# A decoder block on one core: row squares and the FFN's first weights queued behind copies out of PSUM, and layer two's loads queued three products sooner

## The chip, the core and the metric

The kernel runs on one core of a Trainium2 chip. A core has TensorE (matmuls, results in PSUM, eight banks), VectorE (DVE), ScalarE (ACT), GpSimd (POOL) and SyncE (SP), each working through its own queue in order; here nearly all DMAs are issued from SP's queue. PEld is TensorE's loading of the stationary operand, which overlaps its matmuls. The metric is device time of the whole program in microseconds (us), lower is better.

## The reference

One decoder block over 2048 tokens of width 1024, in float32:

```python
hn = rmsnorm(h, norm1_g)
proj = hn @ w_in                       # u_pool | q | k | v, 512 each
y_pool = pool_mixer(u_pool, ...)       # causal means over 2, 4, 8, 16 tokens, then 128x128 maps
o = stick_breaking_attention(q, k, v)  # 8 heads of 64, strictly causal
mixed = concat(rmsnorm(y_pool, pool_out_g), rmsnorm(o, attn_out_g))
h = h + mixed @ w_out
hn2 = rmsnorm(h, norm2_g)
h = h + square(relu(hn2 @ w_up)) @ w_down   # 1024 -> 4096 -> 1024
return rmsnorm(h, final_g)
```

## The kernel before, in words

Tokens are cut into four tiles j = 0 to 3 of T = 512 columns; features lie on the 128 partitions. Every matmul operand is split into a high and a low part (`split`: ScalarE copies the rounded high part, VectorE subtracts for the low part), and each product is three matmuls of 128x512: high-high, high-low, low-high.

The program has these stages:

- **The front** (to some 485 us): two passes over pairs of tiles do the input projection (`in_proj`, `dense`, 24 matmuls for each block of 128 output features, weights `raw` split into `hl` up to five pieces ahead), the pooling mixer and the attention of recent keys. `dense` has two PSUM banks, `pd`; `evac` copies or adds the result out of the bank, on ScalarE or VectorE, and `done` remembers the last two such instructions: `done[1]` is the newest. Copies of v are `vf`, which TensorE then transposes (`ptv`). Attention runs in units woven between the dense products: logits `pz` (two banks), `sh` and `sg` (sigmoids on ScalarE, out of `pz`), a mask by GpSimd, a scan and products on VectorE, transposes `pta`, a split `at`, context matmuls `po`.
- **The squares of x's rows.** The first norm needs mean squares of x's rows. For tiles 1 to 3 they are taken by `row_sums`: a load of 128 rows into the one buffer `rlast`, then a ScalarE square that adds up the row. Four for a tile, twelve in all. For tile 1 all are asked for at once (`n` is 5). For tiles 2 and 3 one step is asked for ahead of an input projection; a step is the square of the last rows and the load of the next.
- **Output projection** (first addition at 487.0 us, last at 672.5): for each tile eight blocks c of 24 matmuls; `add_acc` adds the bank to `acc` on VectorE. At c = 3 of the last tile, `begin_ffn` opens the FFN's buffers and starts `up`.
- **FFN, layer one** (`up`, TensorE's first product at 672.31): Strassen's scheme with seven products P1 to P7 for each pair of halves, 12 matmuls each; stationary operands `hw` from weights `rb` and their sums `rt`, moving operands `sa` from loads `sr` (three buffers) of sums kept in DRAM. `post` brings results out, stores activations to `sd` and sums to `sdi`. Product P2 ends with the store of block A11, P7 with that of A22, P4 with that of S3.
- **FFN, layer two** (`down`, first product at 1285.31): steps of 24 or 48 matmuls; a step loads weights `wr` and one or two operands `ar` and splits them into `wd` and `ad`. `make_ahead` writes steps ahead of their use, up to six operands. Buffers of `ar` are five, two in a pool that the first steps share.

The order on each engine is made by a scheduler that simulates the program as it is written. It may draw an instruction forward wherever its data allow it. `tc.issue_after(ins)` adds an edge without a semaphore: what is written in the block and runs on the same engine as `ins` stays behind `ins` in that engine's queue; on another engine it has no effect. `last_split[0]` is the VectorE half of the newest weight split, `done[1]` may be on either engine, and `marks["A11"]`, `["A22"]` and `["S3"]` are DMAs in SP's queue.

Of the kernel before, what the change touches and what calls it, by code (L numbers as in the profile page):

```python
# [19 lines left out]
NT = S // T  # L20
# [25 lines left out]
def hymba_block(ctx: ExitStack, tc: tile.TileContext, xT, x_rows, gains, w_in, pool_w, w_out, w_up, w_down, out):  # L46
# [110 lines left out]
    marks, gates = {}, []  # L157
    raws, grans, last_split, last_mm, last_load = [], [], [None], [None], [None]
    done = [None, None]
# [168 lines left out]
    def note(emit):  # L328
        prog.append((0, emit, False))
# [53 lines left out]
    def row_sums(j):  # L383

        x = rlast.rearrange("p x t -> p (x t)")
        for b in range(TB + 1):
            if b:
                nc.scalar.activation(x, x, AF.Square, accum_out=sums1[:, j - 1, b - 1:b])
            if b < TB:
                nc.sync.dma_start(x, x_rows[j, b])  # L390
            yield

    row_steps = [iter(())] + [row_sums(j) for j in range(1, NT)]

    def sum_rows(j, n=1):
        for _ in range(n):
            next(row_steps[j])

    def norm1_rms(j):
        st[j]["ss"] = sums1[:, j - 1]  # L400
# [144 lines left out]
    def drained(j):  # L545
        while j not in finished:
            state["due"] = 0.0
            advance(0.1)
# [69 lines left out]
    def tail(first):  # L618

        def root(j):  # L620

            if not (first and j < 2):
                drained(j)
                st[j]["todo"] = attn_norm(j, lambda: make_h(j))

        def mixes(j):
            load_mix(j, KD if first and j < 2 else 4)
            if "todo" in st[j]:
                st[j]["amix"] = st[j].pop("todo")()

        def begin(j):
            catch_up(len(later))
            st[j]["m"] += st[j].pop("amix", [])
            if j > 0:
                norm2(j - 1)
            if j == 2:
                sums_first()

        if first:
            note(to_out)  # L640
        else:
            note(lambda: (root(0), mixes(0), load_acc(0)))
        for j in range(NT):
            if j == 2 and first:
                note(to_last)
            note(lambda j=j: begin(j))
            for c in range(KD):
                if c == 0 and j == 0 and not first:
                    note(lambda: root(1))
                if c == 0 and j + 1 < NT:  # L650
                    note(lambda j=j: mixes(j + 1))
                if c == (2 if j == 0 else 4) and j + 2 < NT:
                    note(lambda j=j: root(j + 2))
                if c == 0 and j == 2:
                    note(lambda j=j: load_acc(j))
                if c == 4 and j in (0, 2):
                    note(lambda j=j: load_acc(j + 1))
                if c == 3 and j == NT - 1:
                    note(begin_ffn)
                wlist.append(w_out[c])  # L660
                step(2, lambda w, j=j, c=c: dense(j, "m", w, lambda ps: add_acc(j, c, ps)))

# [248 lines left out]
    A11, A12, A22, S1, S2, S3, S4 = range(7)  # L911
# [19 lines left out]
    def up(pools, more):  # L931
# [49 lines left out]
        def load(q, m):  # L981
            if q and m % (NM // 2) == NM // 2 - 1:
                raw[q, m] = raw[0, m]
                return
            raw[q, m] = (rbb if m >= NM // 2 else rba).tile([P, 4, G, P], F32, tag="rb", name="rb")
            nc.sync.dma_start(raw[q, m], w_up[m])
# [9 lines left out]
        def make_weights(g):  # L996
            q, m, s = slots[g]
            which, i = what[s][1]
            if s == "P2":
                add_weights(q, m)  # L1000
            hl = hlp.tile([P, 2, G, P], F32R, tag="hw", name="hw", align_bytes=256)
            split((hl[:, 0], hl[:, 1]), (sums if which else raw)[q, m][:, i])
            ops[g] = hl
# [85 lines left out]
        def post(q, m, s):  # L1089
            k = keep.setdefault((q, m), {})  # L1090
            x, y, z = (ps.get((q, m, b)) for b in "XYZ")
            new = lambda name: avp.tile([P, T], F32, tag="av", name=name)

            def put(i, t, kept=None):
                if q == 0 or m >= NM // 2 or i not in INNER:
                    kept = nc.sync.dma_start(sd[q][i][m // 2][:, m % 2], t)
                if q and i in INNER:
                    inner_sums(m, i, t)
                return kept

            def act_of(i, src, t):
                nc.scalar.activation(t, src, AF.Relu)  # L1102
                nc.scalar.activation(t, t, AF.Square)
                k[i] = t

            def copy(name):
                k[name] = pup.tile([P, T], F32, tag=name, name=name)
                nc.scalar.activation(k[name], y, AF.Copy)  # L1108

            if s == "P1":  # L1110
                copy("p1")
            elif s == "P2":
                t = new("a11")
                nc.vector.tensor_tensor(t, x, k["p1"], ALU.add)
                act_of(A11, t, t)
                put(A11, t)
            elif s == "P6":
                if q and m != NM // 2 - 1:
                    for i in INNER:
                        inner_row(m, i)  # L1120
                copy("u2")
            elif s == "P7":
                if q and m == NM // 2 - 1:
                    for i in INNER:
                        inner_row(m, i)
                copy("u3")
                t = new("a22")
                nc.vector.tensor_tensor(t, z, k["u3"], ALU.add)
                act_of(A22, t, t)
                marks["A22"] = put(A22, t)  # L1130
            elif s == "P4":
                t = new("a21")
                act_of("A21", y, t)
                k[S1] = new("s1")
                nc.vector.tensor_tensor(k[S1], t, k[A22], ALU.add)
                put(S1, k[S1])
                k[S2] = new("s2")
                nc.vector.tensor_tensor(k[S2], k[S1], k[A11], ALU.subtract)
                put(S2, k[S2])
                nc.vector.tensor_tensor(t, k[A11], t, ALU.subtract)  # L1140
                marks["S3"] = put(S3, t)
            elif s == "P3":
                t = new("a12")
                nc.vector.tensor_tensor(t, z, k["u2"], ALU.add)  # L1144
                act_of(A12, t, t)
                put(A12, t)
                s4 = new("s4")
                nc.vector.tensor_tensor(s4, t, k[S2], ALU.subtract)
                put(S4, s4)
                while waiting:  # L1150
                    inner_sums(*waiting.pop(0))

        load(*cols[0])
        make_weights(0)
        make_left(0, "P1")
        make_left(0, "P2")
# [9 lines left out]
        for g, (q, m, s) in enumerate(slots):  # L1166
# [7 lines left out]
            n = cols.index((q, m))  # L1174
# [6 lines left out]
            t, w = ps[q, m, bank], ops.pop(g)  # L1181
# [12 lines left out]
            if g + UA < len(slots):  # L1194
                make_weights(g + UA)
                q2, m2, s2 = slots[g + UA]
                n = cols.index((q2, m2)) + 2
# [3 lines left out]
    def down(pools):  # L1201
# [306 lines left out]
        def make_ahead(limit=len(steps)):  # L1508

            while ahead[0] < limit and (ahead[1] + lefts(ahead[0]) <= 6 and ahead[2] + stationary(ahead[0]) <= 3):  # L1510
                make(ahead[0])
                ahead[1] += lefts(ahead[0])
                ahead[2] += stationary(ahead[0])
                ahead[0] += 1

        with tc.high_priority():
            make_ahead(1)
        with tc.issue_after(marks["A22"].ins):
            make_ahead(2)
        with tc.issue_after(marks["S3"].ins):  # L1520
            make_ahead()
        for g, (n_, i, kk, qs_) in enumerate(steps):
            t, left_ = made.pop(g)
# [82 lines left out]
    layer = []  # L1606

    def begin_ffn():
# [17 lines left out]
        layer.append(up([sap, hlp, rba, rtp, srp], more))  # L1626
        next(layer[0])

    def ffn():
        catch_up(len(later))  # L1630
        front_scope.close()
        for _ in layer.pop():
            pass
        left_scope.close()
        with ExitStack() as scope:
            spool = lambda name, bufs, **kw: scope.enter_context(tc.tile_pool(name=name, bufs=bufs, reuse_waits="tile", **kw))

            rlp, pupa = spool("rlp", 2), spool("pupa", 2)
            spool("even", 1).tile([P, 2 * P // 4], F32, name="even")
            rs = spool("rs", 2), spool("rs2", 3)  # L1640
            rt, t8 = spool("rt", 6), spool("t8", DA + 1)
            s8 = spool("s8", 2), spool("s82", 2 * DA - 1)
            tmp2, pup, rtx = spool("tmp2", 2), spool("pup", 6), spool("rtx", 1)
            down([t8, s8, rs, rt, pupa, pup, rtx, rlp, tmp2, spool("psb", 1, space=PS)])
# [22 lines left out]
    tail(True)  # L1667
    run()
    ffn()


# [62 lines left out]
```

## Time and profile before

| what | value |
|---|---|
| median of three runs (lowest, highest) | 1879.13 us (1877.73, 1882.28) |
| the profiled execution | 1876.19 us, of which the span of its instructions 1874.5 |
| TensorE busy, granted clock | 1856.5 us (99% of the span), 0.998 |
| VectorE, ScalarE, GpSimd busy | 1458.1, 1027.6, 218.0 us |
| DMA | 542.20 MB, mean 289 GB/s |
| the squares of rows on ScalarE (L388) | 12, of 1060 ns, from 20.0 to 117.9 us |

The page is one execution. Lines such as L388 are lines of the kernel before; in the changed kernel the same code stands some lines lower (by 4 from `norm1_rms` on, by 6 from the end of `tail`, by 7 from the middle of `up`). In rows of a timeline the columns are start and length in us, engine, line, operation, tiles (output, arrow, inputs), shapes and count; in brackets the engine's idle time before it and what ended it.

### The profile page before, as it was taken

What the parts mean: (1) busy time and instruction counts of PE and PEld (TensorE: products, weight loads), DVE (VectorE), ACT (ScalarE), POOL (GpSimd) and SP (SyncE); (2) the same over time, 40 slices, a digit from 0 to 9 for tenths busy, and PEclk for the clock granted to TensorE, in tenths of its full rate; (3) what the DMA queues carried; (4) which work ended last, traced back from release to release, by engine and by line L of the source; (5) the groups of instructions that cost most, each with busy time, mean ns of one, the idle gap of its engine ahead of it and who ended that gap; (6) DMA issues with size and microseconds to landing.
All of it is one profiled execution on the core that took longest, in us unless ns stands there. A gap on an engine that the chain in (4) does not pass through costs nothing.

```text
span 1874.5 us, 26609 instructions
## 1 busy us (share of the span) xinstructions
PE 1856.5 (99%) x8859; PEld 1549.6 (83%) x8859; DVE 1458.1 (78%) x2100; ACT 1027.6 (55%) x1620; POOL 218.0 (12%) x466
## 2 busy tenths in 40 slices
PE   9999999999999999999999999999999999999997
PEld 7888888888888788888888888887888888888887
DVE  6877798678866877887799988886665677889774
ACT  6655576466544555555566555554333665656643
POOL 1232232213311130000000000000010010020120
PEclk9999999999999999999999999999999999999999
DMA  7986786899796858978798988889999899999862
GB/s 274 300 269 208 232 295 212 272 338 301 271 371 239 303 181 311 342 279 306 277 355 300 330 295 279 284 303 336 375 325 333 272 319 305 331 304 349 287 214 92
DMA packets 223892, 542.20 MB, mean 289 GB/s; under 512 B 26240, under 2 KB 32384, under 8 KB 219904
## 3 DMA queue, kind: packets, MB, share of 16 engines
q1 hardware_dynamic: 218992, 531.75, 81.3%
q0 software_dynamic: 4608, 8.39, 2.5%
q8 instruction: 72, 1.18, 0.3%
q14 instruction: 76, 0.62, 0.1%
q10 hardware_dynamic: 144, 0.26, 0.0%
HBM read 355.75 MB, written 184.55 MB: 288 GB/s over the span
## 4 chain that ended last, share of the span: by engine, by line
PE 94%; DVE 2%; DMA 1%; ACT 1%; issue 0%; SPq 0%; POOL 0%; ACTq 0%; DVEq 0%
PE pY L1185 19%; PE pb L1358 16%; PE pb L1536 12%; PE pZ L1185 9%; PE pd L182 9%; PE pd L183 9%; PE pd L184 8%; PE pX L1185 5%; PE po L739 1%; PE pta L727 1%; PE pr L248 1%; PE pz L680 1%; PE pz L679 1%; PE pm L210 1%; PE pb L1476 0%
## 5 line engine op out<-in xcount | busy, mean ns | idle before, releaser
L1185 PE MATMUL pY<-sa,hw 128*128 128x512 f32 x1536 | 365.2, 389 | 0.7 <-ACT u L1108 0.7
L1185 PEld LDWEIGHTS pY<-sa,hw 128*128 128x128 f32 x1536 | 288.1, 188 | 60.9 <-ACT u L1108 1.1
L1358 PE MATMUL pb<-ad,wd 128*128 128x512 f32 x1344 | 304.8, 389 | 0.0
L182 PE MATMUL pd<-h,hl 128*128 128x512 f32 x752 | 295.1, 392 | 1.9 <-DVE acc L881 1.9
L1358 PEld LDWEIGHTS pb<-ad,wd 128*128 128x128 f32 x1344 | 252.3, 188 | 52.4
L184 PE MATMUL pd<-h,hl 128*128 128x512 f32 x752 | 295.4, 393 | 0.0
L183 PE MATMUL pd<-h,hl 128*128 128x512 f32 x752 | 295.1, 392 | 0.0
L1536 PE MATMUL pb<-ad,wd 128*128 128x512 f32 x1104 | 253.1, 390 | 1.1 <-ACT ad L150 1.0
L1536 PEld LDWEIGHTS pb<-ad,wd 128*128 128x128 f32 x1104 | 206.6, 188 | 44.5 <-ACT ad L150 1.5
L151 DVE TENSOR_TENSOR ad<-ar,ad 128x1024 fp32r<-128x1024 f32 x160 | 194.1, 1221 | 42.2 <-ACT ad L150 41.7
L150 ACT ACTIVATE ad<-ar 128x1024 fp32r<-128x1024 f32 x160 | 168.9, 1057 | 89.0 <-PE pb L1536 31.9
L1185 PE MATMUL pZ<-sa,hw 128*128 128x512 f32 x768 | 185.7, 389 | 0.0
L150 ACT ACTIVATE hl<-raw 128x512 fp32r<-128x512 f32 x168 | 105.6, 631 | 117.2 <-PE pd L184 108.1
L1185 PEld LDWEIGHTS pZ<-sa,hw 128*128 128x128 f32 x768 | 144.1, 188 | 29.9
L182 PEld LDWEIGHTS pd<-h,hl 128*128 128x128 f32 x752 | 141.3, 188 | 28.6 <-issue 2.3
L184 PEld LDWEIGHTS pd<-h,hl 128*128 128x128 f32 x752 | 141.3, 188 | 28.3
L183 PEld LDWEIGHTS pd<-h,hl 128*128 128x128 f32 x752 | 141.4, 188 | 26.8
L151 DVE TENSOR_TENSOR hl<-raw,hl 128x512 fp32r<-128x512 f32 x168 | 115.1, 688 | 44.6 <-ACT hl L150 44.0
L151 DVE TENSOR_TENSOR hw<-rt,hw 128x512 fp32r<-128x512 f32 x128 | 86.9, 687 | 36.0 <-ACT hw L150 35.8
L150 ACT ACTIVATE wd<-wq 128x1024 fp32r<-128x1024 f32 x56 | 59.5, 1063 | 80.4 <-PE pb L1358 71.6
L151 DVE TENSOR_TENSOR wd<-wq,wd 128x1024 fp32r<-128x1024 f32 x56 | 68.5, 1223 | 35.7 <-ACT wd L150 35.7
L1102 ACT ACTIVATE a<-a 128x512 f32<-128x512 f32 x96 | 59.9, 628 | 62.9 <-DVE a L1144 28.1
(235 smaller groups left out, 2684.0 us busy)
## 6 DMA issues: line engine op xcount, KB each, us to landing
ar<-sd SPq DMA_DIRECT2D x96, 512.0 KB, 5.7
ar<-sdi SPq DMA_DIRECT2D x64, 512.0 KB, 5.6
rb<-in_w_up_dram SPq DMA_DIRECT2D x30, 1024.0 KB, 6.9
sd<-a SPq DMA_DIRECT2D x104, 256.0 KB, 4.9
raw<-in_w_in_dram SPq DMA_DIRECT2D x50, 512.0 KB, 4.8
sdi<-hr SPq DMA_DIRECT2D x96, 256.0 KB, 5.4
wr<-in_w_down_dram SPq DMA_DIRECT2D x48, 512.0 KB, 5.7
sd<-s SPq DMA_DIRECT2D x88, 256.0 KB, 4.5
```

Of the source, the lines that this page charges most:

```text
L150: nc.scalar.activation(hi, src, AF.Copy)
L151: return nc.vector.tensor_tensor(lo, src, hi.bitcast(F32), ALU.subtract)
L182: nc.tensor.matmul(ps, hl[:, 0, c], hi, start=(k == 0), stop=False)
L183: nc.tensor.matmul(ps, hl[:, 0, c], lo, start=False, stop=False)
L184: last_mm[0] = nc.tensor.matmul(ps, hl[:, 1, c], hi, start=False, stop=(k == n - 1))
L210: marks["pm"] = nc.tensor.matmul(pm[:, c:c + 1], ss[:, c * P:(c + 1) * P], inv[n], start=(i == 0), stop=(i == len(parts) - 1))
L248: mm = nc.tensor.matmul(pr[:, b * P:(b + 1) * P], yr[:, x, b:b + 1].to_broadcast([P, P]), identr, start=(b == 0 and x == 0), stop=(b == TB ...
L679: nc.tensor.matmul(pz, qa[:, qsl], k, start=first, stop=False, skip_group_check=not (first and last))
L1102: nc.scalar.activation(t, src, AF.Relu)
L1185: nc.tensor.matmul(t, w[:, wx, c], a[:, ax, c % 2], start=first and c == 0 and x == 0, stop=last and c == G - 1 and x == 2, skip_group_che ...
L1358: nc.tensor.matmul(b, t[:, wx, 2 * (kk % 2) + c, i * P:(i + 1) * P], a[:, ax, c], start=p in ("P1", "P5", "P2") and kk == 0 and c == 0 and ...
L1536: nc.tensor.matmul(ps[q, n], block(t, wx, c, n), left_[q][:, ax, c], start=(n_ in ("P1", "P3") and kk == 0 and c == 0 and x == 0), stop=(n ...
```

## The change

Three edits, all of the order of issue; no computation is added or removed.

```diff
     def sum_rows(j, n=1):
         for _ in range(n):
-            next(row_steps[j])
+            with ExitStack() as behind:
+                for ins in (last_split[0], done[1]):
+                    if ins and n == 1:
+                        behind.enter_context(tc.issue_after(ins.ins))
+                next(row_steps[j])
...
                 if c == 3 and j == NT - 1:
                     note(begin_ffn)
+                if c == 4 and j == NT - 1:
+                    note(later_ffn)
...
                 act_of(A11, t, t)
-                put(A11, t)
+                marks["A11"] = put(A11, t)
...
         load(*cols[0])
+        yield
         make_weights(0)
...
         with tc.high_priority():
             make_ahead(1)
+        with tc.issue_after(marks["A11"].ins):
+            make_ahead(2)
         with tc.issue_after(marks["A22"].ins):
-            make_ahead(2)
-        with tc.issue_after(marks["S3"].ins):
             make_ahead()
...
+    def later_ffn():
+        with tc.issue_after(last_split[0].ins), tc.issue_after(done[1].ins):
+            next(layer[0])
+
```

In the front, single steps of the row squares stay behind the newest copy out of PSUM, where that is ScalarE's. Here is ScalarE's queue around the copy `vf` of the second block of v (r, vt, ot, at are other copies and splits; L388 is the square). Before:

```order
L388 ACTIVATE rlast,sums_147<-rlast 128x1024
L150 ACTIVATE at<-pta 128x384
L696 ACTIVATE ot<-po 64x512
L150 ACTIVATE at<-pta 128x512
L388 ACTIVATE rlast,sums_147<-rlast 128x1024
L276 ACTIVATE r<-pr 128x512
L150 ACTIVATE vt<-ptv 128x8x64
L150 ACTIVATE hl<-raw 128x512
L388 ACTIVATE rlast,sums_147<-rlast 128x1024
L493 ACTIVATE vf<-pd 128x512
```

And after, from the same copy r on:

```order
L276 ACTIVATE r<-pr 128x512
L150 ACTIVATE hl<-raw 128x512
L150 ACTIVATE vt<-ptv 128x8x64
L497 ACTIVATE vf<-pd 128x512
L388 ACTIVATE rlast,sums_147<-rlast 128x1024
L150 ACTIVATE hl<-raw 128x512
L702 ACTIVATE ot<-po 64x512
L150 ACTIVATE at<-pta 128x384
L150 ACTIVATE vt<-ptv 128x8x64
L150 ACTIVATE mix<-nt 128x512
L388 ACTIVATE rlast,sums_147<-rlast 128x1024
L691 ACTIVATE sh<-pz 128x384
```

The three squares ahead of `vf` are gone from there; two others (the last of tile 2) now follow it, the second right ahead of an attention unit's `sh`. Tile 3's four moved further down: one pair to the pooling copies of tile 1, one behind the next `vf` of v.

At the start of the FFN, the load of the first `rb` stays at c = 3, and all work on it moves to c = 4, behind the addition of c = 3. VectorE's queue there before, from just behind the first operation on `rb` (L990) to the addition of c = 2:

```order
L151 TENSOR_TENSOR hl<-raw,hl 128x512
L992 TENSOR_TENSOR rt<-rb 128x512
L151 TENSOR_TENSOR hw<-rb,hw 128x512
L991 TENSOR_TENSOR rt<-rb,rt 128x512
L151 TENSOR_TENSOR hw<-rb,hw 128x512
L194 TENSOR_TENSOR sslast<-sslast,sq 128x512
L151 TENSOR_TENSOR hl<-raw,hl 128x512
L993 TENSOR_TENSOR rt<-rb,rt 128x512
L151 TENSOR_TENSOR sa<-sr,sa 128x1024
L218 TENSOR_SCALAR v<-pm 128x4
L151 TENSOR_TENSOR hw<-rt,hw 128x512 x3
L881 TENSOR_TENSOR acc<-pd,acc 128x512
```

After, the additions are L887, of c = 2 and c = 3:

```order
L151 TENSOR_TENSOR hl<-raw,hl 128x512
L194 TENSOR_TENSOR sslast<-sslast,sq 128x512
L151 TENSOR_TENSOR hl<-raw,hl 128x512
L218 TENSOR_SCALAR v<-pm 128x4
L887 TENSOR_TENSOR acc<-pd,acc 128x512
L151 TENSOR_TENSOR hl<-raw,hl 128x512
L194 TENSOR_TENSOR sslast<-sslast,sq 128x512
L151 TENSOR_TENSOR hl<-raw,hl 128x512
L887 TENSOR_TENSOR acc<-pd,acc 128x512
L151 TENSOR_TENSOR hw<-rb,hw 128x512
L151 TENSOR_TENSOR sa<-sr,sa 128x1024 x3
```

Ten operations on `rb`, `rt` and `sr` no longer stand ahead of the addition of c = 2. The splits come after the addition of c = 3 and among the later ones. ScalarE's half of the first two splits keeps its place.

For layer two, SP's queue at the end of layer one, before, from the store of A22 on (sd and sdi are stores, the two `ar` rows are step one's operands):

```order
L1096 DMA sd_2_4_394<-a_13519 128x512
L1245 DMA wr<-in_w_down_dram 128x1024
L954 DMA sdi_0_0_446<-a_13366 128x512
L954 DMA sdi_1_0_450<-hr 128x512
L1096 DMA sd_3_4_402<-s_13545 128x512
L954 DMA sdi_3_0_458<-hr 128x512
L1306 DMA ar<-sd_0_7_325 128x1024
L954 DMA sdi_0_0_462<-s_13413 128x512
L954 DMA sdi_1_0_466<-hr 128x512
L1096 DMA sd_4_4_410<-s_13554 128x512
L1096 DMA sd_5_4_418<-a_13542 128x512
L1306 DMA ar<-sd_0_7_381 128x1024
```

After, from the store of A11 (first row) past that of A22 (sixth row):

```order
L1102 DMA sd_0_4_378<-a_13463 128x512
L1252 DMA wr<-in_w_down_dram 128x1024
L1313 DMA ar<-sd_0_7_325 128x1024
L1313 DMA ar<-sd_0_7_381 128x1024
L1252 DMA wr<-in_w_down_dram 128x1024
L1102 DMA sd_2_4_394<-a_13519 128x512
L1252 DMA wr<-in_w_down_dram 128x1024
L960 DMA sdi_0_0_446<-a_13366 128x512
```

Step one's weights and operands moved ahead of the stores of A22, S1, S2 and A21, and step two's weights stand behind A22's store. Step two's operands stand six and four stores ahead of where they were. VectorE and ScalarE follow: step one's splits now stand among the last sums of layer one, and VectorE's split of step one's weights comes ahead of the addition (L1144) that empties the last bank of layer one.

## The prediction

> **What bounds the kernel now.** I read the page's head first, then the list of TensorE's waits, then the three places that the change touches, each in order of time.
>
> ```profile
> span 1874.5 us, 26609 instructions
> ...
> PE 1856.5 (99%) x8859; PEld 1549.6 (83%) x8859; DVE 1458.1 (78%) x2100; ACT 1027.6 (55%) x1620; POOL 218.0 (12%) x466
> 693.36 5.44 PE pY L1185 x24
> core 0: 1874.5 us, clock 0.998
> ```
>
> TensorE is the bound. 24 of its 512-column matmuls pass in 5.44 us, 0.227 us each, at a granted clock of 0.998. The change removes no matmul, so it can only move the gaps between them.
>
> ```profile
> PE pd L182 <- DVE acc L881: 1.9, 1, 1.9
> ...
> PE ptv L496 <- ACT vf L493: 1.5, 1, 1.5
> PE pb L1536 <- ACT ad L150: 1.0, 1, 1.0
> ```
>
> These are the waits in question (total us, times, longest): L496 in the front, L182 at the start of the FFN, L1536 in layer two. The records draw a matmul 0.39 us long though the next may follow after 0.227, so the true loss is 0.16 us above the row.
>
> **The front: squares behind copies.** ScalarE squares x's rows in one buffer, `rlast`, so a square waits for its load, and the next load for that square. Of the loads' own line (L390) the first row, then SP, ScalarE and TensorE in time:
>
> ```profile
> DMA to landing us min/median/max: 3.6/5.6/9.4
> 107.98 0.36 SPq L390 DMA_DIRECT2D rlast<-in_x_rows_dram  x1
> 106.58 1.06 ACT L388 ACTIVATE rlast<-rlast 128x1024 f32<-128x1024 f32 x1 [3.42 <-DMA rlast<-in_x_rows_dram]
> ...
> 113.08 1.06 ACT L388 ACTIVATE rlast<-rlast 128x1024 f32<-128x1024 f32 x1 [3.73 <-DMA rlast<-in_x_rows_dram]
> 117.88 1.06 ACT L388 ACTIVATE rlast<-rlast 128x1024 f32<-128x1024 f32 x1 [2.15 <-DMA rlast<-in_x_rows_dram]
> 118.93 0.58 ACT L493 ACTIVATE vf<-pd 128x512 f32<-128x512 f32 x1
> 110.83 0.66 PE L496 MATMUL ptv<-ident,vf 128*128 128x128 f32 x4 [0.37 <-DVE vf L491]
> 117.76 0.31 PE L679 MATMUL pz<-kw,qa 128*128 128x128 f32 x1
> 119.56 0.66 PE L496 MATMUL ptv<-ident,vf 128*128 128x128 f32 x4 [1.50 <-ACT vf L493]
> ```
>
> Before, ScalarE sat 2.15 us for a load with the copy `vf` queued behind, and TensorE stood from 117.81 (the short pz matmul takes 0.05) to 119.56: 1.75 us. The same kind of wait at 106.58 delayed VectorE's `vf` and cost 0.53 (0.37 and the 0.16). By the new order `vf` goes ahead of the square, and both gaps, 2.28 us, go.
>
> The squares go elsewhere, though. Six of the twelve keep their place. Of the other six, one stands right behind `vf`, its load long landed; the next is five copies later, ahead of `sh` and `sg` of an attention unit; the last four are in the next part of the front. Where two follow closely, the second must wait for a load that starts only when the first is done. First place, with TensorE's new order: the dense product that `vf` copies ended some 0.7 ahead of the pz row at 117.76; less 0.53, and one product that now stands later, that is 116.2. `vf` runs to 117.0, the square to 118.1, the load is issued at 118.2. This load's time is unknown; the ends are 3.6 and 9.4 and I take 5.1 (107.98 to 113.08), the same tile's load nearest in time that found the queue as busy. So it lands at 123.3, the square ends at 124.5, `sh` and `sg` at 125.4. Then come the mask on POOL and the products on VectorE:
>
> ```profile
> 122.43 0.50 ACT L687 ACTIVATE sg<-pz 128x384 f32<-128x384 f32 x1
> 123.01 1.74 POOL L710 TENSOR_SCALAR_AFFINE_SELECT sg<-sg 128x256 f32<-128x256 f32 x1 [13.95 <-ACT sg L687]
> 124.78 0.63 DVE L717 TENSOR_TENSOR sg<-sg,pc 128x127 f32<-128x127 f32 x2 [0.24 <-POOL sg L710]
> 127.17 0.49 PE L727 MATMUL pta<-ident,sg 128*128 128x128 f32 x3
> ```
>
> From the end of `sg` (122.93) to the end of L717 (125.41) took 2.5, so the transposes pta can start at about 127.8. TensorE's new order wants them at 125.5 (from 117.9, where logits follow ptv, 25 dense products, 5.7, and 2.0 of short ones). New gap: 2.3 us, or L minus 2.8 for a landing time L; 0.8 at 3.6, 6.6 at 9.4. On POOL the row sums' root now stands ahead of that mask; its accumulator is ready at 124.5, so it costs the mask no more than half a microsecond, within the 2.3.
>
> Second place, j = 1's pooling copies:
>
> ```profile
> 182.06 0.60 ACT L427 ACTIVATE u<-pd 128x512 f32<-128x512 f32 x1 [1.32 <-PE pd L184]
> 190.65 0.40 PE L452 MATMUL pp<-pls,pw 128*128 128x512 f32 x1
> ```
>
> A square behind `u` runs from 182.7 to 183.9, the next load lands at 184 + L, then a square of 1.25 and the copy `yb` (0.6) free the bank that L452 needs at 191.3 (190.65 and three matmuls that now stand ahead): a gap of L - 5.4, nothing at 5.1. The third place, some 25 us later (a square behind the next `vf`), I put at L - 6.1 by the same reckoning: nothing. Later squares cost ScalarE no more work, and their sums have until the next norm. Front: 2.28 - 2.3, nothing gained; ends +1.5 (L = 3.6) and -11.6 (9.4 three times: 6.6 + 4.0 + 3.3, less 2.3).
>
> The Trainium skill (DMA: Bandwidth & Descriptors, section Anatomy of one DMA) puts a DMA, fitted on GpSimd's, at a fixed 2.0 us plus bytes over 436 GB/s; by that an estimate for these 512 KB is 3.2 us, the first gap would be 0.4 and the front would gain 1.9. The fastest of the twelve here took 3.6 and the median 5.6, so the trace does not agree and the sum goes by the rows.
>
> **The FFN's first weights.** In the output projection's last turn VectorE and ScalarE reach the work on `rb` before it has landed.
>
> ```profile
> 632.53 0.33 SPq L986 DMA_DIRECT2D rb<-in_w_up_dram  x1
> 641.15 0.69 DVE L990 TENSOR_TENSOR rt<-rb 128x512 f32<-128x512 f32 x1 [3.69 <-DMA rb<-in_w_up_dram]
> 649.59 0.68 DVE L881 TENSOR_TENSOR acc<-pd,acc 128x512 f32<-128x512 f32 x1
> 648.13 0.39 PE L184 MATMUL pd<-h,hl 128*128 128x512 f32 x1
> 650.42 0.47 PE L182 MATMUL pd<-h,hl 128*128 128x512 f32 x1 [1.91 <-DVE acc L881]
> 651.43 1.46 SPq L1009 DMA_DIRECT2D sr<-su  x2
> 655.66 1.07 ACT L150 ACTIVATE sa<-sr 128x1024 fp32r<-128x1024 f32 x1 [1.51 <-DMA sr<-su]
> 647.79 1.88 DVE L151 TENSOR_TENSOR hw<-rt,hw 128x512 fp32r<-128x512 f32 x3
> ...
> 654.87 1.21 DVE L151 TENSOR_TENSOR sa<-sr,sa 128x1024 fp32r<-128x1024 f32 x1
> ```
>
> The addition out of PSUM (L881) of c = 2 waited behind that work until 649.59; TensorE lost 650.42 - 648.13 - 0.23 = 2.06 us. The new order has this L881, and the next, ahead of all the weights' splits. Gone: 2.06. What is late next: the same splits now stand between later additions. A split of 512 columns takes 0.6 of VectorE (three in 1.88), one of 1024 takes 1.14 (the pair in layer two below in 2.35, less 1.21). From 648.6: L881 of c = 3, one split of 0.6, three of 1.14, six operations of 0.6, L881 of c = 4 done at 657.4 (wanted 659.2); then five of 0.6 and three of 1.14 to 663.8, and L881 of c = 5, whose bank frees 0.8 later (as from 649.59 to 650.42), 664.6. TensorE wants that bank at 648.36 + 3 x 5.44 = 664.7. That is even, so I take 0.15 off: **1.9**. The loads on SP that move behind additions (`sr`, three buffers) land in 4.2 (651.43 to 655.66); three microseconds more would stop VectorE ahead of c = 5 and give the 2.06 back. Ends: +2.06 and -0.8.
>
> **Layer two's loads.** Steps one and two (counted from zero) of layer two:
>
> ```profile
> 1286.52 1.03 SPq L1306 DMA_DIRECT2D ar<-sd  x1
> ...
> 1301.07 1.84 SPq L1306 DMA_DIRECT2D ar<-sd  x2
> 1307.17 1.06 ACT L150 ACTIVATE ad<-ar 128x1024 fp32r<-128x1024 f32 x1 [6.58 <-DMA ar<-sd]
> 1285.31 21.92 PE L1536 MATMUL pb<-ad,wd 128*128 128x512 f32 x96
> 1308.28 1.99 PE L1536 MATMUL pb<-ad,wd 128*128 128x512 f32 x6 [1.04 <-ACT ad L150]
> 1278.04 2.35 DVE L151 TENSOR_TENSOR ad<-ar,ad 128x1024 fp32r<-128x1024 f32 x2
> 1287.71 0.68 DVE L1144 TENSOR_TENSOR a<-pZ,u 128x512 f32<-128x512 f32 x1
> ```
>
> Steps zero and one fill 1285.31 to 1307.07 (96 x 0.227); step two started at 1308.28, 1.21 late, for a load issued at 1301.07. That load reuses the buffers of step one's, which came late because SP, in order, had stores ahead that waited for VectorE. Step one's loads went out from 1286.52 on. Now they follow the store of A11, issued from about 1281 (their buffers come free when VectorE ends step zero's splits at 1280.4), and land near 1288. Their splits end by 1294, step two's loads go out by 1294 between the remaining stores and land near 1300, seven microseconds before they are wanted. The price: VectorE splits step one's weights ahead of L1144, which empties a bank that step zero's fourth-to-seventh products want from 1290.7. Should those weights take 7 us from 1280.6, L1144 ends at 1290.7, just in time. I take **1.2**; ends 1.2 and -0.5. Two squares on ScalarE and the sums after them slip some 2.5 us; nothing near reads them.
>
> **Sum.** 0.0 + 1.9 + 1.2 = 3.1 us. The profiled execution took 1876.19 (span 1874.5 and 1.7 around it) and should take 1873.1. It was quicker than all three runs shown (1877.73 to 1882.28, median 1879.13), so on their scale: 1879.13 - 3.1 = **1876.0**.
>
> **Rivals.**
> 1. The loads land quickly or the squares' cover is better than I count (speaks for it: 3.6 us for the last load; against: the median of 5.6). All four gaps go: 2.28 + 2.06 + 1.21 = 5.55, 1873.6. More is not in the trace, and this is just under 0.3%, 5.6 us, about what a measurement of this kernel can tell from no change.
> 2. Slower: ScalarE stands at the moved squares with copies out of PSUM behind them. The three gaps add up to 3L - 14.3. To be 5.6 us slower they must reach 5.6 + 3.1 + 2.3 = 11.0, that is L = 8.4 at all three places; 9.4 was seen once and 5.6 is the median. Price at L = 8.4: 1884.7.
> 3. A gap so long slows the clock as well. At the start TensorE ran its first products 0.43 us apart:
>
> ```profile
> 8.34 0.63 PE L525 MATMUL pd<-h,hl 128*128 128x512 f32 x1
> 8.77 0.63 PE L526 MATMUL pd<-h,hl 128*128 128x512 f32 x1
> ```
>
>    After an idle stretch it may do so again for some microseconds: eight products at 0.43 instead of 0.227 are 1.6 us. With one gap of 3.9 (L = 6.7) the front loses 3.9 + 1.3 + 0.6 + 1.6 - 2.3 = 5.1, and the whole, with 3.1 gained elsewhere, ends at 1881.1. No wait here was over 1.91 us, and the clock stayed at 0.998. The Trainium skill (TensorE: Matmul & The Clock Gate, section What's actually happening) halves the clock after an idle window of about 3.4 us; no run here shows it for a gap inside the kernel.
> 4. The change hardly acts: the gaps at c = 2 and step two only move, to c = 5 (the even sum above) and to the bank of L1144: 1878.5 to 1879.
>
> **Chances.** Forecast case, 1874.5 to 1878: 0.58. Rival 1: 0.14. Rival 4: 0.17. Rival 3: 0.06. Rival 2: 0.05. Faster by over 0.3% needs rival 1 and a lucky median, 0.07; slower by as much is rival 2, 0.05; the rest is the same, 0.88. The range takes in rival 1's better part, the forecast and rival 4, with the scatter of the runs shown: 1873.0 to 1880.5.
>
> **What would show it.** Right: no wait of ptv for `vf` in the front, but ScalarE waiting for `rlast` ahead of `sh` near 121 and TensorE's pta for the masked `sg` behind it; no wait of pd for the addition near 650; step two following step one at 0.227. Wrong: a wait of pd for the addition near 664, or of step zero for L1144; ScalarE never idle at the moved squares (rival 1); or a gap of over 3 us in the front.

## The result, and the profile after

The changed kernel takes 1883.11 us (median of 13 runs, 1881.42 to 1886.59), the kernel before in the same comparison 1878.61 (13 runs, 1876.2 to 1882.28). The ratio is 1.0026, with a 95% interval from 1.0018 to 1.0034: some 4.9 us slower, where 3.1 less were forecast. 1883.11 lies above the predicted range. The profiled execution took 1882.4 us.

TensorE's list of waits of the changed kernel, top and the rows that bear on the change (total us, times, longest), ahead of it the head of the page and the clock:

```profile
span 1880.4 us, 26609 instructions
core 0: 1880.4 us, clock 0.996
PE pr L248 <- POOL yrlast L894: 6.7, 1, 6.7
PE pzero L364 <- DVE zero L94: 1.5, 1, 1.5
...
PE pd L182 <- DVE qk L151: 0.6, 1, 0.6
...
PE pb L1365 <- DVE ad L151: 0.5, 1, 0.5
...
PE po L745 <- DVE ot L703: 0.4, 1, 0.4
```

All three waits that the prediction named (ptv for `vf`, pd for the addition, pb for `ad` ahead of step two) are gone. The small waits in the list (`qk`, `ad`, `ot`) are new and come to 1.5 us together. A single new one takes more than all the old ones gave: L248 is `spread`, which turns the roots of the second norm into rows on all partitions, and in layer one it does so for tiles 2 and 3 (products 6 and 10 of `up`; `yrlast` is what POOL's chain of roots writes). TensorE in time at that place, after:

```profile
684.24 1.00 PE L248 MATMUL pr<-identr,yrlast 128*128 128x128 f32 x8
685.08 0.67 PE L1192 MATMUL pX<-sa,hw 128*128 128x512 f32 x2
692.43 0.48 PE L248 MATMUL pr<-identr,yrlast 128*128 128x128 f32 x1 [6.68 <-POOL yrlast L894]
692.71 5.32 PE L1192 MATMUL pY<-sa,hw 128*128 128x512 f32 x12
```

Eight matmuls of the first spread, two of a product, and then one alone, the first of tile 3's spread, for which TensorE stands from 685.6 to 692.4. The twelve matmuls behind it take 5.32 us where twelve took 2.88 elsewhere. The same engine by stretches (the column after the busy shares is the granted clock):

```profile
693.00:694.00 1.00, 1.00 (x3) 0.81 (x3) 0.00 (x0) 0.00 (x0) 0.00 (x0) 0.50 0.00 0
...
698.00:699.00 1.00, 1.00 (x6) 0.80 (x5) 0.31 (x1) 0.94 (x2) 0.00 (x0) 1.00 0.00 0
```

TensorE is as busy as ever there, at half the clock: three or four matmuls in a microsecond, then six. So the place costs 6.84 us of gap (start to start, less the pair's usual distance) and 2.5 of slow matmuls.

Why the one matmul waits so long: POOL's chain of roots for tile 3, and VectorE beside it, both after.

```profile
681.17 7.59 POOL L219 TENSOR_SCALAR v<-v 128x4 int32<-128x4 int32 x1 [32.96 <-DVE v L218]
688.84 0.20 POOL L226 TENSOR_TENSOR v<-v 128x4 f32<-128x4 f32 x1
...
692.19 0.19 POOL L894 CAST yrlast<-v 128x4 fp32r<-128x4 f32 x1
```

```profile
680.93 0.15 DVE L218 TENSOR_SCALAR v<-pm 128x4 f32<-128x4 f32 x1
681.00 0.68 DVE L996 TENSOR_TENSOR rt<-rb 128x512 f32<-128x512 f32 x1
...
687.42 1.29 DVE L151 TENSOR_TENSOR hw<-rt,hw 128x512 fp32r<-128x512 f32 x2
```

An operation on four columns is drawn 7.59 us long and ends at 688.76, just as VectorE comes to the end (688.71) of ten operations without a break, all with both inputs in SBUF. For tile 2 the same operation, after a longer idle stretch and beside an addition with one input in PSUM (L887), took 0.20:

```profile
642.97 0.20 POOL L219 TENSOR_SCALAR v<-v 128x4 int32<-128x4 int32 x1 [50.28 <-DVE v L218]
```

Before, TensorE had all eight matmuls of this second spread together further down, when the roots were long there (first row POOL, then TensorE):

```profile
680.45 6.38 POOL L219 TENSOR_SCALAR v<-v 128x4 int32<-128x4 int32 x1 [17.65 <-DVE v L218]
704.07 1.00 PE L248 MATMUL pr<-identr,yrlast 128*128 128x128 f32 x8
```

So the slow operation on POOL was there already, ending at 686.83 where VectorE's run of eight ended at 686.77, and nothing waited for it. What changed is TensorE's queue. Its rows from the first spread on, before and then after:

```
L248 MATMUL pr<-identr,yrlast 128x128 x8
L1185 MATMUL pX<-sa,hw 128x512 x2
L1185 MATMUL pY<-sa,hw 128x512 x12
L1185 MATMUL pX<-sa,hw 128x512 x10
L1185 MATMUL pY<-sa,hw 128x512 x24
L1185 MATMUL pZ<-sa,hw 128x512 x24
L248 MATMUL pr<-identr,yrlast 128x128 x8

L248 MATMUL pr<-identr,yrlast 128x128 x8
L1192 MATMUL pX<-sa,hw 128x512 x2
L248 MATMUL pr<-identr,yrlast 128x128
L1192 MATMUL pY<-sa,hw 128x512 x12
L1192 MATMUL pX<-sa,hw 128x512 x10
L1192 MATMUL pY<-sa,hw 128x512 x24
L1192 MATMUL pZ<-sa,hw 128x512 x24
L248 MATMUL pr<-identr,yrlast 128x128 x7
```

One matmul of 128 columns was drawn forward past 70 others. It is the first of the eight and reads only what the cast (L894) wrote; the second reads what POOL's last operation (L895, the rest behind the cast) wrote. This suggests that the scheduler's simulation had the cast done by then and that operation not yet; this is argued from the order, not shown.

### The profile page after: what moved, and what is told of

It is laid out like the page before. It is cut to its first block, busy times and chain, and to the rows that moved or that the text cites. A ratio compares the mean times of both kernels' runs of the same rounds, so it can differ in the third digit from the quotient of the medians.

```text
span 1880.4 us, 26609 instructions
## 1 busy us (share of the span) xinstructions
PE 1858.1 (99%) x8859; PEld 1550.2 (82%) x8859; DVE 1457.2 (77%) x2100; ACT 1027.8 (55%) x1620; POOL 212.9 (11%) x466
## 4 chain that ended last, share of the span: by engine, by line
PE 88%; DMA 4%; DVE 4%; issue 1%; POOL 1%; ACT 1%; SPq 0%; ACTq 0%; DVEq 0%; POOLq 0%
PE pY L1192 18%; PE pb L1365 14%; PE pb L1543 13%; PE pZ L1192 9%; PE pd L182 7%; PE pd L184 7%; PE pd L183 7%; PE pX L1192 4%; PE po L745 1%; PE pta L733 1%; DMA xt<-in_xT_dram 1%; DMA sr<-su 1%; DMA ar<-sdi 1%; DMA ar<-sd 1%; PE pr L248 1%
## 5 line engine op out<-in xcount | busy, mean ns | idle before, releaser
L1192 PE MATMUL pX<-sa,hw 128*128 128x512 f32 x384 | 93.7, 389 | 0.0
```

What stands on the lines that cost most here:

```text
L1192: nc.tensor.matmul(t, w[:, wx, c], a[:, ax, c % 2], start=first and c == 0 and x == 0, stop=last and c == G - 1 and x == 2, skip_group_che ...
```

## The experiments

Theory A: the loss is this one matmul, and edit two (the FFN's first weights) puts it there. Rival B: POOL's chain is late for the stage, so whatever reads it waits. Rival C: it takes the front or layer two as well. Ratios are to the kernel before on the same chip, with 95% intervals.

| run | kernel | median us | ratio |
|---|---|---|---|
| a1_held | whole change, spread held | 1874.70 | 0.9979 (0.9968 to 0.9989) |
| a2_edit2 | FFN's first weights alone | 1885.86 | 1.0042 (1.0027 to 1.0057) |
| a3_edits13 | front and layer two | 1874.44 | 0.9976 (0.9967 to 0.9985) |
| a4_edit3 | layer two alone | 1877.30 | 0.9993 (0.9982 to 1.0005) |
| b1_edit1 | front alone | 1876.79 | 0.9991 (0.9982 to 0.9999) |
| c3_held_no_front | FFN's weights, layer two, spread held | 1875.79 | 0.9987 (0.9977 to 0.9996) |

**a1_held.** In `up`, with `marks["hold"]` the last matmul of product 10:

```diff
             elif g in (6, 10):
                 pr, i = psu.tile([P, T], F32, tag="R", name="pr"), g // 10
-                spread(pr, yrlast[:, i])
+                with tc.issue_after(marks["hold"].ins) if i else nullcontext():
+                    spread(pr, yrlast[:, i])
```

> The whole change, with the second tile's spread of the roots held behind the products of its own place, so that its first matmul cannot stand ahead in TensorE's queue; nothing else moves. Theory A (the loss is one matmul drawn forward, that waits for POOL's root): the 6.84 us gap at 685.4 and the half-clock stretch behind it (2.4 us) go, the span falls from 1880.4 to 1871 (9.3 less), 3.5 below before's 1874.5, ratio to before 0.998. Rival B (the root chain on POOL is itself late for the stage, so whatever reads it next waits): a gap of several us appears at the spread's later place or at its reader, span 1876 to 1880.

In TensorE's queue the single L248 is back with its seven, and from the first spread on the rows are in the order of the kernel before. TensorE at the place, and POOL:

```profile
685.40 1.00 PE L248 MATMUL pr<-identr,yrlast 128*128 128x128 f32 x8
686.25 0.67 PE L1192 MATMUL pX<-sa,hw 128*128 128x512 f32 x2
686.78 3.06 PE L1192 MATMUL pY<-sa,hw 128*128 128x512 f32 x12
```

```profile
682.63 7.58 POOL L219 TENSOR_SCALAR v<-v 128x4 int32<-128x4 int32 x1 [33.14 <-DVE v L218]
```

POOL's operation is as slow as in the changed kernel and costs nothing. The gap and the half clock are gone, no wait for `yrlast` appears (one of 1.1 us for ScalarE's `sa` does, at 985), and the span is 1873.0. That is theory A, and against B. With this the change is 0.0021 faster than before, some 3.9 us, and it beats both kernels (as a3_edits13 does, below).

**a2_edit2, a3_edits13.** Edit two alone, and edits one and three without it.

```diff
# a3_edits13, against the changed kernel
-                if c == 4 and j == NT - 1:
-                    note(later_ffn)
...
         load(*cols[0])
-        yield
         make_weights(0)
```

> Before with only the FFN's first weights moved; here too the first matmul of the second spread stands ahead in TensorE's queue. Theory A: the 2.07 us gap near 648 goes (+2.1) and the one at 685 with its slow stretch comes (-9.3): 7 us slower than before, ratio 1.004, as slow as the whole change or 1 us slower. Rival C (the loss needs the front's moved squares or layer two's loads as well): within 2 us of before, ratio 0.999 to 1.001.

> Front's squares and layer two's loads moved, the FFN's first weights as before; the spread stands whole in its place. Theory A: no gap near 685 or 690; the front gains 0.5 us or less, layer two 0.7 to 1.2, the 2.07 us gap near 648 stays: span 1873 to 1874, ratio 0.9993 to 1.0. Rival C: the gap near 685 is there as well and the ratio is over 1.003.

The top of TensorE's waits, of a2_edit2 and then of a3_edits13:

```profile
PE pr L248 <- POOL yrlast L890: 6.5, 1, 6.5
```

```profile
PE pd L182 <- DVE acc L885: 1.8, 1, 1.8
```

Edit two by itself brings the wait, with the slow stretch behind it, and 1.0042: rival C falls. Without it the wait is not there. a3_edits13 came out better than expected (0.9976 for 0.9993 to 1.0). The front alone and layer two alone, which follow, give 0.0009 and 0.0007 of that; the rest lies within the intervals.

**a4_edit3, b1_edit1, c3_held_no_front.** One edit alone, and a1_held without the front's.

```diff
# c3_held_no_front, against a1_held
-            with ExitStack() as behind:
-                for ins in (last_split[0], done[1]):
-                    if ins and n == 1:
-                        behind.enter_context(tc.issue_after(ins.ins))
-                next(row_steps[j])
+            next(row_steps[j])
```

> Before with only layer two's loads moved. By my sum: the 1.20 us gap between steps one and two goes and nothing takes its place, span 1873.3, ratio 0.9994. By the trace of the changed kernel, where a new wait of 0.63 us for VectorE stands later in layer two: 0.5 to 0.7 less, 1873.9, ratio 0.9997.

> Before with only the front's squares held behind the copies. By my sum: nothing gained in the front, ratio 1.000 (0.9995 to 1.0005). If the difference between the runs with edits one and three (0.9976) and three alone (0.9993) is the front's: ratio 0.998. No gap near 685 in either case, and the two waits of ptv for vf gone.

> The run a1 without the front's squares (edits two and three, spread held). If the front's edit is worth the 0.0009 that it showed alone, ratio to before 0.9988; if edits two and three carry a1's 0.9979 by themselves, 0.998; if the three only pay together, 0.999 to 1.0.

Layer two alone is 0.0007 faster, on the forecast but not told from nothing by its interval. The front alone gives 0.0009, which is neither the nothing of my sum nor the 0.002 of the other expectation. a1_held with it is 0.0008 better than c3_held_no_front without it, about 1.5 us, and a3_edits13 is 0.0017 better than a4_edit3, about 3.2. None of these differences is far outside the intervals, but all three have the same sign. Of the three expectations for c3, the first is met (0.9988 expected, 0.9987 measured).

**b2_gap_3_9, b3_gap_3_2, c2_gap_short, d1_gap_1.** How long must the gap be to slow the clock? The whole second spread stands behind matmul k of product 8, k = 2, 5, 8, 11, so that TensorE comes to it later (each of the four ran once, and its rows are read, not its time):

```diff
+                    if (g, 3 * c + x) == (8, 2):
+                        pr = psu.tile([P, T], F32, tag="R", name="pr")
+                        with tc.high_priority(), tc.issue_after(mm_.ins):
+                            spread(pr, yrlast[:, 1])
+                        nc.scalar.activation(rlast[:, 1], pr, AF.Copy)
...
-            elif g in (6, 10):
+            elif g == 6:
```

> The whole change, with the second spread put 13 products behind the place where its first matmul stood (12 of pY and one of pX), so that TensorE arrives there 13 x 0.227 = 2.95 us later and the gap for POOL's root shrinks from 6.8 to 3.9 us. Clock by length of the gap (a stretch of some microseconds without matmuls halves it): as long a half-clock stretch behind it as behind 6.8 (some 12 matmuls 0.43 apart, 2.4 us lost) if 3.9 is long enough, none if only longer gaps do it. Rival (it is the waiting matmul or what follows it, not the gap's length): the slow stretch is there whatever the gap.

> As the run before, three products later: gap 3.2 us. Estimate from the Trainium skill (TensorE: Matmul & The Clock Gate, section What's actually happening, an idle window of about 3.4 us): no half-clock stretch, matmuls 0.227 apart right behind the spread. Rival: 12 slow matmuls here too.

> The whole change with the second spread 19 products behind the place where its first matmul stood: three fewer than b3's 16 left 2.4 us of gap, so about 1.7. If the clock falls after gaps of 2.4 us and more but not after 2.07 (none in the kernel before): no half-clock stretch, span about 1873 to 1875. Rival: a stretch here too, so it does not hang on the gap's length.

> The whole change with the second spread 22 products behind the place where its first matmul stood: 19 left 1.74 us of gap and a half-clock stretch of 1.7 us lost, so this gap is about 1.1. If the gap's length decides in the end: no half-clock stretch, 1.1 us lost there. Rival (the sixteen short matmuls of the two spreads near each other slow the clock by themselves): a stretch of 0.43 here too; against it, the kernels that hold the spread in its place have none.

The spread and the matmuls behind it in b2, b3, c2 and d1, in this order:

```profile
693.00 2.03 PE L248 MATMUL pr<-identr,yrlast 128*128 128x128 f32 x8 [4.05 <-POOL yrlast L894]
694.83 4.15 PE L1192 MATMUL pX<-sa,hw 128*128 128x512 f32 x9
```

```profile
693.08 1.27 PE L248 MATMUL pr<-identr,yrlast 128*128 128x128 f32 x8 [2.25 <-POOL yrlast L894]
694.19 2.53 PE L1192 MATMUL pX<-sa,hw 128*128 128x512 f32 x6
```

```profile
692.56 1.35 PE L248 MATMUL pr<-identr,yrlast 128*128 128x128 f32 x8 [1.58 <-POOL yrlast L894]
693.71 1.59 PE L1192 MATMUL pX<-sa,hw 128*128 128x512 f32 x3
```

```profile
693.34 1.28 PE L248 MATMUL pr<-identr,yrlast 128*128 128x128 f32 x8 [2.32 <-POOL yrlast L894]
694.45 3.89 PE L1192 MATMUL pY<-sa,hw 128*128 128x512 f32 x16
```

At 0.227 apart nine matmuls are drawn 2.2 us long, six 1.5, three 0.85 and sixteen 3.8. So behind the gap of 4.2 us the nine run at half clock; behind 2.4, in b3, the slow stretch comes too, from 694.6 to 698.0; behind 1.7 it comes as well; behind 2.5, in d1, it does not. Both of my expectations on the shorter gaps were wrong, and so was d1's gap: its chain on POOL ended 0.8 us later than c2's, and TensorE got to the place 0.6 earlier. A gap's length alone does not settle it.

Where the gap lies explains it. The traces record when the granted clock changed, and in each of the twelve traces of the block all its changes stand whole multiples of 3.413 us apart (in the changed kernel 682.67, 10.24 and 1177.60 us, which is 200, 3 and 345 times). So the clock is set in fixed windows of that length. Three windows of c2, of which the first holds its gap whole, and then the slow one of a3_edits13 (the granted clock is again the column after the busy shares):

```profile
690.20:693.62 3.42, 1.84 (x12) 1.28 (x11) 1.15 (x2) 1.61 (x3) 1.95 (x8) 1.00 0.19 75
693.62:697.03 3.41, 3.41 (x10) 2.74 (x10) 0.69 (x1) 1.23 (x2) 0.00 (x0) 0.50 0.01 2
697.03:700.44 3.41, 3.41 (x16) 2.79 (x16) 0.00 (x0) 0.57 (x2) 0.00 (x0) 1.00 0.00 0
...
651.37:654.78 3.41, 3.41 (x10) 2.63 (x9) 3.41 (x6) 1.59 (x2) 3.33 (x2) 0.50 0.88 266
```

| kernel | gap of TensorE, us | part of it in the window ahead of the drop; without a drop, the largest part in one window | half clock, us |
|---|---|---|---|
| the changed one | 685.6 to 692.4 | 1.93 | 687.5 to 697.8 |
| b2_gap_3_9 | 688.8 to 693.0 | 3.41 | 692.6 to 699.4 |
| b3_gap_3_2 | 690.7 to 693.1 | 1.93 | 694.6 to 698.0 |
| c2_gap_short | 690.8 to 692.6 | 1.74 | 693.6 to 697.0 |
| a3_edits13 (the old gap at c = 2) | 648.6 to 650.6 | 2.00 | 651.4 to 654.8 |
| d1_gap_1 | 690.9 to 693.3 | 1.61 | none |
| before (c = 2) | 648.4 to 650.4 | 1.16 | none |
| before (the front) | 117.9 to 119.6 | 1.7 | none |

A window's end at 692.47 divided d1's gap into 1.61 and 0.87. So every drop here followed a window that held 1.74 us or more of a gap, and the longer gaps without a drop were divided by a window's end. The front's gap of 1.7 in the kernel before lay whole in one window and brought no drop: c2's 1.74 is close to the limit, and what exactly the windows count is open. The Trainium skill (TensorE: Matmul & The Clock Gate, section What's actually happening) has activity judged over free-running windows of 3.4 us, which do not start with the gap; the traces agree, with 3.413. But the idle window of about 3.4 us, by which I set b3's expectation, need not be idle throughout: 1.74 us of it was enough in c2.

**b4_port, c1_port_free.** Is POOL's operation slow because of VectorE? Sixteen additions on VectorE, with POOL's chain beside them:

```diff
+            if kind == "sbuf":
+                for i in range(16):
+                    nc.vector.tensor_tensor(zs[i], x, y, ALU.add)
+            elif kind == "psum":
+                for i in range(16):
+                    nc.vector.tensor_tensor(zs[16 + i], pd, y, ALU.add)
```

(In b4 all write one tile, `z`.)

> Not the block: twelve of POOL's operations on 128x4 (as in the root's chain) beside sixteen VectorE additions of 128x512 that follow each other without a break, first with both inputs in SBUF, then with one in PSUM, then with VectorE idle; the output is a constant. Theory D (POOL's small operation cannot start while VectorE runs operations with two SBUF inputs back to back): beside the first kind POOL's chain ends only after all sixteen, its first operation drawn 9 to 10 us long; beside the second kind and alone each takes 0.2 us and the chain 3.4. Rival E (POOL's first operation after an idle stretch is slow, whatever VectorE does): the first operation is drawn long in all three.

> As the run b4, with each of VectorE's sixteen additions writing a tile of its own, so that they follow each other as in the block (0.60 us apart instead of 0.72, no break between them); the output is a constant. Theory D: beside additions with both inputs in SBUF, POOL's chain does not get in between them: one operation drawn some 9 us long, ending when the additions end; beside additions with one input in PSUM 0.2 us each. Rival (POOL gets in once per VectorE operation whatever the breaks): 0.65 us each, as in b4.

VectorE and then POOL in c1:

```profile
2.47 9.71 DVE L66 TENSOR_TENSOR z<-x,y 128x512 f32<-128x512 f32 x16
12.17 9.64 DVE L69 TENSOR_TENSOR z<-pd,y 128x512 f32<-128x512 f32 x16
```

```profile
2.69 0.51 POOL L71 TENSOR_TENSOR v<-v 128x4 f32<-128x4 f32 x1 [2.26 <-DVE v L62]
3.28 0.53 POOL L72 TENSOR_TENSOR v<-v 128x4 f32<-128x4 f32 x1
...
12.34 0.20 POOL L71 TENSOR_TENSOR v<-v 128x4 f32<-128x4 f32 x1 [2.51 <-DVE v L62]
```

Beside additions with two inputs in SBUF each of POOL's operations takes 0.51 to 0.53 us and gets in once per addition (0.65 in b4, where they stand 0.72 apart); beside additions with one input in PSUM, and with VectorE idle, 0.20. So VectorE's two SBUF inputs do hold POOL up, and an idle stretch before it does not (rival E falls; in the block, too, tile 2's L219 took 0.20 after 50.28 us). But theory D's size falls as well: alone, POOL waits for one addition, not for all sixteen. The Trainium skill (SBUF — State Buffer, section SBUF: two separate sides) has the two engines share one pair of ports, held for a whole instruction; the runs agree with that, with 0.51 to 0.53 us beside two SBUF inputs for 0.20 beside one. In the block two more long operations of the kernel before, tile 2's L219 (1.77 us) and L228 (4.03), ended 0.14 and 0.13 us after VectorE had started an addition with an input in PSUM (649.59 and 654.27). Why POOL did not get in between the operations ahead of that, as it did in c1, stays open, and so it does for L219's 7.59 us.

## Why the prediction was wrong, point by point

What each stage lost can be read over all twelve profiles of the block: from each matmul's start to the next, less the usual distance for its shape, summed up by stretches of the span (us, mean, differences taken before rounding; "with" and "without" is the edit that acts there).

| stretch | without | with | difference | forecast |
|---|---|---|---|---|
| 100 to 130 (front's squares) | 2.1 (4 kernels) | 0.6 (8) | -1.5 | 0.0 |
| 0 to 640 (all ahead of the FFN's weights) | 8.0 (4) | 8.1 (8) | +0.2 | 0.0 |
| 640 to 684 (FFN's first weights) | 2.1 (4) | 0.6 (8) | -1.4 | -1.9 |
| 1250 to 1320 (layer two) | 2.6 (3) | 1.2 (9) | -1.4 | -1.2 |
| 684 to 700 in the changed kernel | 0.0 | 9.5 | +9.5 | 0 |

- **The step that failed is the sum**, which had no term for TensorE's own queue in layer one. Edit two's part asked what is late next on VectorE, ScalarE and SP, whose work it moves, and took TensorE's order of the products as fixed. The order of TensorE's queue showed the L248 row out of its place; I read past it, because no edit names that line. Priced by the rows of before it would have given a wait of some 4 us: L218 ends at 680.4, L219 takes 6.38 and the rest of the chain some 3.5, which is 690.3, and TensorE, at that place at 688.2 before, would come 1.9 earlier. The runs show 6.84, because L218 ended at 681.1, L219 took 7.59 and TensorE came at 685.6, and 2.5 of half clock on top.
- **Rival 3's mechanism came, at another place.** The clock does halve behind a gap inside the kernel, and 2.5 us for it is more than the 1.6 I put. I gave it 0.06, in the front only, and against it "no wait here was over 1.91 us". That was no bar even in the old order: in a3_edits13 the old wait at c = 2, of 1.8 us, brought 3.41 us of half clock.
- **The front** was mis-sized. The feared wait at the mask did not come. ScalarE and SP after:

```profile
114.88 0.60 ACT L497 ACTIVATE vf<-pd 128x512 f32<-128x512 f32 x1 [2.09 <-PE pd L184]
115.38 1.05 ACT L388 ACTIVATE rlast<-rlast 128x1024 f32<-128x1024 f32 x1
...
119.56 0.63 ACT L150 ACTIVATE mix<-nt 128x512 fp32r<-128x512 f32 x1
120.26 1.06 ACT L388 ACTIVATE rlast<-rlast 128x1024 f32<-128x1024 f32 x1
121.32 0.47 ACT L691 ACTIVATE sh<-pz 128x384 f32<-128x384 f32 x1
```

```profile
116.54 0.33 SPq L390 DMA_DIRECT2D rlast<-in_x_rows_dram  x1
```

  `vf` ran 1.5 us earlier than I reckoned, and the load took at most 3.7 us (116.54 to 120.26) where I took 5.1; the second square went without waiting. At the place itself the means gain 1.5 us (100 to 130), but over all 640 us nothing of it is left in them; single executions with the front's edit differ by up to 2.9 us there. The timed runs say 1.5 to 3.2. How much the front gives in the end is open.
- **FFN's first weights**: the gap went as forecast, but its size was one execution's. It hangs on the load of `rb`. Of the four executions with the old order here, VectorE waited 3.63 to 3.85 us for that load in three (a3_edits13, the kernel before, b1_edit1), and TensorE's gap was 2.0 to 2.2; in a4_edit3 the wait was 1.60 (first row of VectorE on `rb` below), and there was no gap. In a3_edits13 the gap brought the half clock as well. The even sum at c = 5 did show, as 0.5 to 0.8 us near 664 in some kernels (in the changed one not at all). In the timed runs the gain is not to be told from nothing: a1_held has 0.9979 with this edit, a3_edits13 0.9976 without.

```profile
638.73 0.69 DVE L990 TENSOR_TENSOR rt<-rb 128x512 f32<-128x512 f32 x1 [1.60 <-DMA rb<-in_w_up_dram]
```

- **Layer two**: right. Step two follows step one without a gap:

```profile
1292.41 52.98 PE L1543 MATMUL pb<-ad,wd 128*128 128x512 f32 x233
```

- The three terms together were 3.1 us; the whole change with the spread held gives 3.9 (0.0021 of 1878). That the two are near is in part luck: by the timed runs the front gave something where I had put nothing, and the 1.9 of the FFN's weights does not show.

## What to carry to other kernels

When a scheduler sets the order, a change moves instructions that no edit names: go through the whole difference on the bounding engine, above all for a lone instruction drawn ahead of its group, and price each against the time at which its data really come. An instruction whose input comes from an engine that the scheduler may time wrongly should be held behind its own place's work; that one edit turned a loss of 4.9 us into a gain of 3.9. When an edit fails, time each part alone and look at the single new wait before giving up the change: here the parts other than edit two gave 0.0024 by themselves.

## What the hardware showed that I had not expected

- A 128x4 operation on POOL took 6.38 to 7.59 us beside an unbroken run of eight to ten VectorE operations with two SBUF inputs in this kernel, 0.51 to 0.53 beside sixteen such additions in a row in c1, and 0.20 beside an addition with one input in PSUM.
- In all twelve traces the granted clock changed only at the ends of fixed windows of 3.413 us, and within the run it fell to 0.50 only behind windows that held 1.74 us or more of a gap of TensorE. Gaps of 2.1 and 2.5 us that a window's end divided brought no drop.
- At half clock the matmuls stood 0.43 us apart for 0.227, so by estimate 3.41 us of it, as in b3, cost 1.6 us, and the 6.4 that TensorE worked through in b2 cost 3.0.
